# Weight splits after the norms, transfers on another queue and a norm factor applied later, in a two-part transformer on one core

## The chip, the cores and the metric

The kernel runs on one NeuronCore of a Trainium2 chip. Its engines are TensorE (PE: matmuls and their weight loads), VectorE (DVE), ScalarE (ACT) and GpSimd (POOL). SyncE (SP) only issues transfers; GpSimd, ScalarE and SyncE each have a queue of transfers that are issued in order. The metric is the device time of one execution in microseconds (us); the time of a kernel is the median of its runs.

## The reference

One sequence of 256 tokens of width 1024 goes through two layers (differential attention with PEER, then stick-breaking attention with PEER), then through one block of a second network, all in fp32. Cut to the parts that the change touches:

```python
def _layer_norm(x, g, b):
    mu = jnp.mean(xf, axis=-1, keepdims=True)
    var = jnp.mean(jnp.square(xf - mu), axis=-1, keepdims=True)
    return (xf - mu) * lax.rsqrt(var + LN_EPS) * g + b

def rms_norm(x, gain):
    return xf * lax.rsqrt(jnp.mean(xf * xf, axis=-1, keepdims=True) + NORM_EPS) * gain

# first_block, for each of two layers:
    x = _layer_norm(DEEPNORM_ALPHA * x + mix, ln_g[layer, 0], ln_b[layer, 0])
    ffn = _peer(x, ...)              # per token: 128 of 16384 experts, h = gelu(x . u_e), sum of gate h v_e
    x = _layer_norm(DEEPNORM_ALPHA * x + ffn, ln_g[layer, 1], ln_b[layer, 1])

# second_block:
    u = rms_norm(h, attn_pre_norm[l])
    mix = hybrid_mixer(u, ...)       # w_in, attention with rotary step, a recurrence, w_out
    h = h + rms_norm(mix, attn_post_norm[l])
    u = rms_norm(h, mlp_pre_norm[l])
    m = jnp.square(jax.nn.relu(u @ w_mlp_up[l])) @ w_mlp_down[l]
    h = h + rms_norm(m, mlp_post_norm[l])
```

## The kernel before

**Tiles and splits.** All weights come as tiles of 128x1024 fp32 (512 KB). `Stream` loads them in the order of use, on SyncE's queue, into a ring of four raw buffers (L50), and splits each into two rounded parts: `hi`, a copy on ScalarE (L66), and `lo`, the rest, on VectorE (L67). Activations are split the same way (`part`, L163 and L164), and each product is three matmuls, hi·hi, hi·lo and lo·hi (L157 to L159 in `mm3`, L182 in `mm_n`). `next()` hands out a tile and first asks for loads three tiles ahead and for splits two tiles ahead, more if `extra` is set. A split needs a buffer of the parts pool, which has three, or a buffer of its own, which `keep` gives to named tiles. The engines run in program order: the place of `next()` in the code fixes where a split stands on VectorE and ScalarE.

**PEER.** It is computed densely: 128 tiles of `peer_u` give the scores and hidden values of all experts, then a v loop of 128 iterations (in `peer`) takes one tile of `peer_v` each, makes the iteration's weights (`weigh`, L856, and their two parts `wh` and `wo`) and adds to four accumulators in PSUM: two blocks b of 128 tokens by two halves of 512 columns. From iteration GSPLIT = 112 on, tiles may have buffers of their own. In the last DEFER = 6 iterations only the matmuls of block 0 run; those of block 1 are held and run afterwards, while block 0 is normalised. `proj_n`, the other projection onto the model's width, defers in the same way.

**The junction between two stages.** When block 0's accumulators are done, `layer_norm` runs `norm` for block 0: sum with the residual (L305), statistics, centring and gain (L313), root (`rsqrt`), x (L316). TensorE transposes the result (`transposed`, L289), and ScalarE and VectorE split the transposed x into `xh` and `xl`. Then `half_pass(0)` runs block 0 through the first four tiles of the next stage (NJ = 4, the junction tiles; each is used twice, so each has a buffer of its own), 24 matmuls, while block 1 is normalised; its transposes and `half_pass(1)` over the same tiles follow. The four `next()` calls stand in `half_pass(0)`. With `after`, a pre-norm follows the norm at once; so it is after the second PEER, where block 2 begins.

**Block 2.** `proj_n` with w_out ends in the same kind of junction, written out in `block2`: `post_norm` (squares of the accumulator on ScalarE L908, product with the gain L938, root, x = x + u·r at L942), then `pre_norm` of the new x (squares, products with the gain L921 and L923, root, scaling L925), transposes, half passes. x is stored to DRAM at L1208 and loaded again at L1218 into memory that becomes free after the half passes. The MLP has 32 tiles of `w_up`; each projection goes through a relu on ScalarE (L1237), a square and a split. `proj_n` with w_down and a last `post_norm` write `out`.

**What sets the order.** The schedule is written by hand: each engine and each queue runs in the order of the code. Loads of x, gains, masks, keys, cos and sin, and the stores of x between the stages (`spill`), are issued on SyncE's queue, in a row with the weight tiles. A transfer there is issued when all before it have been and when its buffer is free.

## Time and profile before

| | before |
|---|---|
| median of 3 runs | 2309.69 us (2308.02 to 2313.12) |
| the profiled execution | 2311.31 us |
| its span in the trace | 2309.2 us |
| mean granted TensorE clock | 0.988 |
| TensorE busy | 2230.4 us, 97% |
| VectorE, ScalarE, GpSimd busy | 76%, 54%, 3% |
| DMA | 479.85 MB, mean 208 GB/s |

The span reaches from the first to the last instruction of the profiled execution; 2.1 us of its time lie around it. Busy times are shares of the span. Where TensorE stands still, the timeline shows it as a bracket at the next instruction: how long the engine was idle before it, and whose work it waited for.

### The profile page before, as it was taken

To read this page: it belongs to the slowest core of one execution; us is meant where nothing else is said; L and a number is where in the kernel's file an instruction comes from. 1 tells how busy PE (TensorE), PEld (TensorE's weight loads), DVE (VectorE), ACT (ScalarE), POOL (GpSimd) and SP (SyncE) were. 2 spreads that over 40 slices of the span, in tenths; PEclk is the share of its full clock that TensorE was granted. 3 is DMA by queue.
4 is the path that set the end of the run, shared out by engine and by line. 5 is a ranking of instruction groups with operands and counts; after the bars stand their busy time and mean duration, and the time that the engine had idled before them with its cause. 6 is when DMAs were issued, how large, how long until landed. Compare 5 with 4: busy or idle time off the path is not lost.

```text
span 2309.2 us, 39787 instructions
## 1 busy us (share of the span) xinstructions
PE 2230.4 (97%) x15028; PEld 2011.0 (87%) x15028; DVE 1752.8 (76%) x3488; ACT 1237.7 (54%) x2128; POOL 58.3 (3%) x79
## 2 busy tenths in 40 slices
PE   7889999999999999999999999999999899998998
PEld 6769999999888888887999999888888779997987
DVE  5968999888766767576998988766666856676754
ACT  4545454666555444584445566655444546755543
POOL 5400000000000000000000000000000000000000
PEclk9999999999999999999999999999999999999999
DMA  6336667555777777545666655677777564464764
GB/s 209 120 129 226 226 228 241 191 200 203 259 241 259 241 245 252 167 132 179 229 228 229 226 191 201 234 241 243 258 244 249 199 194 149 137 206 142 227 195 142
DMA packets 150657, 479.85 MB, mean 208 GB/s; under 512 B 17728, under 2 KB 18624, under 8 KB 149184
## 3 DMA queue, kind: packets, MB, share of 16 engines
q1 hardware_dynamic: 131456, 442.69, 59.1%
q10 hardware_dynamic: 19008, 34.61, 4.0%
q8 instruction: 118, 1.93, 0.3%
q14 instruction: 75, 0.61, 0.1%
HBM read 437.39 MB, written 39.85 MB: 207 GB/s over the span
## 4 chain that ended last, share of the span: by engine, by line
PE 85%; DVE 6%; ACT 4%; DMA 2%; issue 2%; POOL 1%; SPq 0%; DVEq 0%; ACTq 0%; POOLq 0%
PE ps_acc L182 34%; PE ps_h L157 15%; PE ps_h L159 14%; PE ps_h L158 14%; DVE lo L67 2%; PE ps_acc L805 1%; PE ps_acc L806 1%; ACT hi L66 1%; PE ps_acc L158 1%; PE ps_acc L159 1%; PE ps_acc L157 1%; DMA raw<-w_up 1%; PE ps_acc L689 0%; DVE aa L469 0%; POOL swq L418 0%
## 5 line engine op out<-in xcount | busy, mean ns | idle before, releaser
L67 DVE TENSOR_TENSOR lo<-raw,hi 128x1024 fp32r<-128x1024 f32 x740 | 904.9, 1226 | 454.2 <-ACT hi L66 451.8
L66 ACT CAST hi<-raw 128x1024 fp32r<-128x1024 f32 x740 | 775.4, 1050 | 437.3 <-issue 308.6
L157 PE MATMUL ps_h<-xh,hi 128*128 128x256 f32 x2784 | 790.3, 284 | 5.0 <-ACT r L1237 2.2
L159 PE MATMUL ps_h<-xh,lo 128*128 128x256 f32 x2784 | 774.3, 278 | 1.3 <-DVE lo L67 1.1
L158 PE MATMUL ps_h<-xl,hi 128*128 128x256 f32 x2784 | 774.4, 278 | 0.0
L157 PEld LDWEIGHTS ps_h<-xh,hi 128*128 128x128 f32 x2784 | 526.5, 189 | 11.8 <-ACT r L1237 2.4
L159 PEld LDWEIGHTS ps_h<-xh,lo 128*128 128x128 f32 x2784 | 525.1, 189 | 2.3 <-DVE lo L67 2.3
L158 PEld LDWEIGHTS ps_h<-xl,hi 128*128 128x128 f32 x2784 | 525.3, 189 | 0.2
L182 PE MATMUL ps_acc<-hi,wh 128*128 128x512 f32 x1024 | 315.4, 389 | 3.3 <-ACT wh L163 3.3
L182 PE MATMUL ps_acc<-hi,wo 128*128 128x512 f32 x1024 | 315.4, 389 | 0.0
L182 PE MATMUL ps_acc<-lo,wh 128*128 128x512 f32 x1024 | 315.1, 389 | 0.0
L832 ACT ACTIVATE hs<-ps_h 128x256 f32<-128x256 f32 x256 | 98.3, 384 | 344.1 <-PE ps_h L159 176.2
L182 PEld LDWEIGHTS ps_acc<-hi,wh 128*128 128x128 f32 x1024 | 192.1, 188 | 43.5 <-ACT wh L163 3.6
L182 PEld LDWEIGHTS ps_acc<-hi,wo 128*128 128x128 f32 x1024 | 192.3, 188 | 39.9
L182 PEld LDWEIGHTS ps_acc<-lo,wh 128*128 128x128 f32 x1024 | 192.3, 188 | 39.7
L164 DVE TENSOR_TENSOR wo<-jd,wh 128x256 fp32r<-128x256 f32 x256 | 107.2, 419 | 2.0 <-ACT wh L163 2.0
L856 DVE TENSOR_TENSOR jd<-G,jd 128x256 f32<-128x256 f32 x256 | 106.9, 418 | 2.2 <-ACT G L808 2.2
L163 ACT CAST wh<-jd 128x256 fp32r<-128x256 f32 x256 | 101.7, 397 | 10.4 <-DVE jd L856 10.4
L808 ACT ACTIVATE G<-ps_acc 128x64 f32<-128x64 f32 (+1 forms) x256 | 82.0, 385 | 6.6 <-PE ps_acc L806 1.0
L157 PE MATMUL ps_h<-hi,xh 128*128 128x512 f32 x160 | 70.8, 442 | 11.8 <-ACT hi L66 9.8
L158 PE MATMUL ps_h<-lo,xh 128*128 128x512 f32 x160 | 67.9, 424 | 5.7 <-DVE lo L67 5.7
L159 PE MATMUL ps_h<-hi,xl 128*128 128x512 f32 x160 | 68.0, 425 | 2.5 <-DVE xl L164 2.5
(323 smaller groups left out, 2384.3 us busy)
## 6 DMA issues: line engine op xcount, KB each, us to landing
raw<-peer_u SPq DMA_DIRECT2D x256, 512.0 KB, 4.5
raw<-peer_v SPq DMA_DIRECT2D x256, 512.0 KB, 4.3
H<-hs SPq DMA_DIRECT2D x128, 256.0 KB, 2.1
jd<-H ACTq DMA_DIRECT2D x128, 256.0 KB, 4.2
raw<-w_in SPq DMA_DIRECT2D x32, 512.0 KB, 3.7
raw<-w_up SPq DMA_DIRECT2D x32, 512.0 KB, 4.4
raw<-w_down SPq DMA_DIRECT2D x32, 512.0 KB, 3.7
raw<-w_qkv SPq DMA_DIRECT2D x24, 512.0 KB, 4.5
```

The lines of the kernel that those rows point to most:

```text
L66: self.nc.scalar.copy(hi, raw)
L67: self.nc.vector.tensor_sub(lo, raw, hi)
L157: mm(out, lh, rh, start=start, stop=False)
L158: mm(out, lh, rl, start=False, stop=False)
L159: mm(out, ll, rh, start=False, stop=stop)
L163: self.nc.scalar.copy(hi, src)
L164: self.nc.vector.tensor_sub(lo, src, hi)
L182: mm(acc[half], x, w[:, half * 512 : half * 512 + 512], start=a, stop=b)
L805: mm(out, o[:, 0, j], o[:, 1, j], start=True, stop=False)
L808: nc.scalar.activation(gt[:, :, 4 * g : 4 * g + 4], ps.rearrange("p (t i) -> p i t", t=4)[:, first:end], AF.Copy, scale=1.0 / GSCALE,)
L832: nc.scalar.activation(hs[i // 2][:, i % 2], o, AF.Gelu)
L856: nc.vector.tensor_tensor(w, g[:, i - first], hl[i // 2][:, i % 2], ALU.mult)
```

## The change

Five edits, in the code's order.

- **Splits.** In `half_pass(0)` tiles are taken with `next(calm=True)`, which splits no further than the tile itself; the splits of tiles after the junction move into `half_pass(1)`, one for each tile but the first. One split more is written between the transposes of block 0 and the half pass in `layer_norm` and `block2`. In `peer`'s last 16 iterations and in the last ones of `proj_n`, `extra` rises to 2, so that more junction tiles are split ahead of the norm.
- **Held matmuls** (`finish`): block 1's held jobs run one half of the columns after the other, where before both halves ran job by job.
- **`norm`**: the second half is centred after x of the first half.
- **Queues**: the loads of x, gains, masks, keys, cos, sin and the stores to `spill` are issued on GpSimd's queue. Weight tiles and `out` stay on SyncE's.
- **Block 2's inner norm**: `pre_norm` before the MLP is replaced by the product with its gain, made half by half (`then`). The row factor r of that norm is left out of u; as relu and square follow, the MLP's output lacks r². `late_norm`, after the second half pass, computes r² from x into `factor`, and the last `post_norm` takes it through `by`: as the scale of its squares and as an operand in `rsqrt`.

```diff
-    def next(self):
+    def next(self, calm=False):
...
-        self.split(i + 1 + self.split_ahead + self.extra, i)
+        self.split(i + 1 if calm else i + 1 + self.split_ahead + self.extra, i)
...
+    def finish(self, held):
+
+        for half in range(2):
+            for job in held:
+                self.mm_n(*job, (half,))
...
-            self.st.extra = max(0, min(2, NJ * (k + 2 - count + defer) // defer))
+            self.st.extra = max(0, min(2, k - count + 6))
...
-        for job in held:
-            self.mm_n(*job)
+        self.finish(held)
...
             if b == 0:
-                tiles.append(self.st.next())
+                tiles.append(self.st.next(calm=True))
+            elif j:
+                self.st.split(self.st.used + j, self.st.used)
...
-        nc.vector.tensor_tensor(out, y, z, ALU.mult)
+        if by is None:
+            nc.vector.tensor_tensor(out, y, z, ALU.mult)
+        else:
+            nc.vector.scalar_tensor_tensor(out, y, by, z, ALU.mult, ALU.mult)
...
-        self.nc.sync.dma_start(t, src.unsqueeze(0).to_broadcast([P, D]))
+        self.nc.gpsimd.dma_start(t, src.unsqueeze(0).to_broadcast([P, D]))
...
-        for s in halves:
-            nc.vector.scalar_tensor_tensor(y[:, s], y[:, s], mv[:, 0:1], g[:, s], ALU.subtract, ALU.mult)
...
+        centre(halves[0])
         next(root)
         for s in halves:
+            if s is halves[1]:
+                centre(s)
             nc.vector.scalar_tensor_tensor(x[:, b, s], y[:, s], r, beta[:, s], ALU.mult, ALU.add)
...
+        self.st.split(self.st.used + NJ, self.st.used)
         next(n1)
         self.half_pass(0, tiles)
...
-            nc.sync.dma_start(x, a["x"].rearrange("(b p) d -> p b d", p=P))
+            nc.gpsimd.dma_start(x, a["x"].rearrange("(b p) d -> p b d", p=P))
...
+                if i >= GSPLIT:
+                    self.st.extra = min(2, (i - GSPLIT) // 4)
                 hi, lo = self.st.next()
...
+            nc.scalar.activation(junk, halves[h], AF.Square, scale=1.0 if by is None else by, accum_out=ss[:, h : h + 1])
...
+    def late_norm(self, pool, x, square):
+
+        r = pool.tile([P, 1], F32, tag="lt_r", name=f"ltr{self.n}", bufs=2)
+        yield from self.mean_square(pool, r, [x[:, :512], x[:, 512:]], 1e-6)
+        self.nc.vector.tensor_tensor(square, r, r, ALU.mult)
+        yield
...
             for b in range(NB):
-                self.post_norm(two, acc[b], x[:, b], gains[0])
-                u = self.pre_norm(two, x[:, b], gains[1])
+                u = two.tile([P, D], F32, tag="ln_y", name=f"lnu{b}", bufs=2)
+                scaled = lambda s: nc.vector.tensor_tensor(u[:, s], x[:, b, s], gains[1][:, s], ALU.mult)
+                self.post_norm(two, acc[b], x[:, b], gains[0], then=scaled)
                 for h in range(2):
                     self.transposed(b, h, u)
                 if b == 0:
+                    self.st.split(self.st.used + NJ, self.st.used)
                     self.half_pass(0, tiles)
             self.half_pass(1, tiles)
-            nc.sync.dma_start(spill, x)
+            for b in range(NB):
+                for _ in self.late_norm(two, x[:, b], factor[:, b : b + 1]):
+                    pass
+            nc.gpsimd.dma_start(spill, x)
```

The places at which the order of instructions moves. A row is a line of the kernel, an operation, and out<-in by tile names; numbers at the names count the tiles.

VectorE at the end of the first PEER, from the end of block 1's norm on, before (`lnr`: the norm's root; `xr0`: x; `lo298`, `lo299`: splits of the third and fourth junction tile; `lo300`, `lo301`: of the two tiles after them; `xl`: the split of the transposed x):

```order
L264 TENSOR_TENSOR lnr304_10673<-rsy307_10694,rsz307_10695 128x1
L316 SCALAR_TENSOR_TENSOR xr0_9141<-lny304_10670,lnr304_10673,gains301_10278 128x512 x2
L67 TENSOR_TENSOR lo298_10710<-raw298_10596,hi298_10709 128x1024
L67 TENSOR_TENSOR lo299_10722<-raw299_10707,hi299_10721 128x1024
L67 TENSOR_TENSOR lo300_10734<-raw300_10719,hi300_10733 128x1024
L67 TENSOR_TENSOR lo301_10746<-raw301_10731,hi301_10745 128x1024
L164 TENSOR_TENSOR xl_72<-ps_m310_10755,xh_71 128x4x128
L164 TENSOR_TENSOR xl_72<-ps_m311_10762,xh_71 128x4x128
```

and now, from the last iteration of the v loop (`wo0127`) to the first sums of block 0's norm (`lny302`), and again from the end of block 1's norm on:

```order
L164 TENSOR_TENSOR wo0127_10578<-jd_73,wh0127_10577 128x256
L67 TENSOR_TENSOR lo298_10597<-raw298_10594,hi298_10596 128x1024
L67 TENSOR_TENSOR lo299_10609<-raw299_10606,hi299_10608 128x1024
L316 SCALAR_TENSOR_TENSOR lny302_10658<-xr0_9141,ps_acc297_7633 128x512
...
L329 SCALAR_TENSOR_TENSOR xr0_9141<-lny304_10680,lnr304_10683,gains301_10278 128x512
L323 SCALAR_TENSOR_TENSOR lny304_10680<-lny304_10680,lnm304_10682,gains301_10278 128x512
L329 SCALAR_TENSOR_TENSOR xr0_9141<-lny304_10680,lnr304_10683,gains301_10278 128x512
L164 TENSOR_TENSOR xl_72<-ps_m310_10747,xh_71 128x4x128
L164 TENSOR_TENSOR xl_72<-ps_m311_10754,xh_71 128x4x128
L67 TENSOR_TENSOR lo300_10769<-raw300_10723,hi300_10768 128x1024
L67 TENSOR_TENSOR lo301_10779<-raw301_10731,hi301_10778 128x1024
```

The third and fourth junction tiles (`lo298`, `lo299`), split after block 1's norm before, are now split before block 0's, and the splits of the tiles after the junction stand behind the split of x.

VectorE at block 2's inner norm, block 0, before (`qnu`, `qnr`: the outer norm; `pnu`, `pnr`, `mss`, `rsx`, `rsz`: the inner norm, its root and sums; `lo680`, `lo681`: splits):

```order
L942 SCALAR_TENSOR_TENSOR x2_23751<-qnu750_24209,qnr750_24208,x2_23751 128x512 x2
L921 TENSOR_TENSOR pnu751_24229<-x2_23751,gains736_23753 128x512
L910 TENSOR_TENSOR mss751_24231<-mss751_24231 128x1
L260 TENSOR_SCALAR rsx751_24236<-mss751_24231 128x1
L923 TENSOR_TENSOR pnu751_24229<-x2_23751,gains736_23753 128x512
L262 SCALAR_TENSOR_TENSOR rsz751_24238<-rsy751_24237,rsx751_24236 128x1
L263 TENSOR_SCALAR rsz751_24238<-rsz751_24238 128x1
L264 TENSOR_TENSOR pnr751_24228<-rsy751_24237,rsz751_24238 128x1
L925 TENSOR_SCALAR pnu751_24229<-pnu751_24229,pnr751_24228 128x512
L164 TENSOR_TENSOR xl_72<-ps_m753_24248,xh_71 128x4x128
L164 TENSOR_TENSOR xl_72<-ps_m754_24255,xh_71 128x4x128
L67 TENSOR_TENSOR lo680_24280<-raw680_24269,hi680_24279 128x1024
```

and now (`lnu0`: x times the inner norm's gain):

```order
L966 SCALAR_TENSOR_TENSOR x2_23755<-qnu750_24214,qnr750_24213,x2_23755 128x512
L1230 TENSOR_TENSOR lnu0_24212<-x2_23755,gains736_23757 128x512
L966 SCALAR_TENSOR_TENSOR x2_23755<-qnu750_24214,qnr750_24213,x2_23755 128x512
L1230 TENSOR_TENSOR lnu0_24212<-x2_23755,gains736_23757 128x512
L164 TENSOR_TENSOR xl_72<-ps_m752_24235,xh_71 128x4x128
L164 TENSOR_TENSOR xl_72<-ps_m753_24242,xh_71 128x4x128
L962 TENSOR_TENSOR qnu754_24282<-ps_acc749_24056,gains736_23757 128x512
```

The inner norm's sums and root are gone, x and its product with the gain alternate by halves, and no split stands before block 1's outer norm (`qnu754`).

SyncE's queue around the end of block 2's junction, before (`raw`: weight tiles; `xs`: x in DRAM; `x3`: the MLP's copy):

```order
L50 DMA raw680_24269<-w_up2 128x1024
L50 DMA raw681_24277<-w_up2 128x1024
L50 DMA raw682_24289<-w_up2 128x1024
L1208 DMA xs_1657<-x2_23751 128x2048
L1218 DMA x3_24396<-xs_1657 128x2048
L270 DMA gain760_24398<-mlp_post_norm_2 128x1024
L50 DMA raw683_24401<-w_up2 128x1024
L50 DMA raw684_24437<-w_up2 128x1024
```

and now on SyncE's queue and, behind it, what is on GpSimd's from block 2's load of x to the end:

```order
L50 DMA raw680_24256<-w_up2 128x1024
L50 DMA raw681_24264<-w_up2 128x1024
L50 DMA raw682_24272<-w_up2 128x1024
L50 DMA raw683_24407<-w_up2 128x1024
L50 DMA raw684_24439<-w_up2 128x1024
```

```order
L1209 DMA x2_23755<-xs_1661 128x2048
L288 DMA gains736_23757<-attn_post_norm_2 128x1024
L288 DMA gains736_23757<-mlp_pre_norm_2 128x1024
L1241 DMA xs_1661<-x2_23755 128x2048
L1251 DMA x3_24402<-xs_1661 128x2048
L281 DMA gain760_24404<-mlp_post_norm_2 128x1024
```

The store and the load of x and the load of the gain no longer stand between the weight tiles `raw682` and `raw683`.

## Rows read from the trace of the kernel before

**Rows 1.** The page's busy times: us, share of the span, instructions.

```profile
PE 2230.4 (97%) x15028; PEld 2011.0 (87%) x15028; DVE 1752.8 (76%) x3488; ACT 1237.7 (54%) x2128; POOL 58.3 (3%) x79
```

**Rows 2.** Timeline, TensorE after layer 0: start, us, what, [idle before <-releaser].

```profile
141.27 0.72 PE L182 MATMUL ps_acc<-hi,oh 128*128 128x512 f32 x2 [2.14 <-ACT oh L163]
...
150.67 1.82 PE L289 MATMUL ps_m<-ident,x 128*128 128x128 f32 x8 [2.29 <-DVE x L316]
...
162.01 0.50 PE L159 MATMUL ps_h<-hi,xl 128*128 128x512 f32 x1 [1.09 <-DVE xl L164]
```

**Rows 3.** Timeline, TensorE after the first PEER and after layer 1.

```profile
929.33 0.50 PE L157 MATMUL ps_h<-hi,xh 128*128 128x512 f32 x1 [1.53 <-ACT hi L66]
932.44 0.73 PE L158 MATMUL ps_h<-lo,xh 128*128 128x512 f32 x1 [2.60 <-DVE lo L67]
...
1065.93 0.50 PE L159 MATMUL ps_h<-hi,xl 128*128 128x512 f32 x1 [1.41 <-DVE xl L164]
```

**Rows 4.** Timeline, TensorE after the second PEER and at block 2's start.

```profile
1828.98 1.09 PE L289 MATMUL ps_m<-ident,pnu 128*128 128x128 f32 x8 [1.68 <-DVE pnu L925]
...
1838.27 0.79 PE L158 MATMUL ps_h<-lo,xh 128*128 128x512 f32 x1 [2.61 <-DVE lo L67]
...
1844.25 1.06 PE L289 MATMUL ps_m<-ident,pnu 128*128 128x128 f32 x8 [0.93 <-DVE pnu L925]
...
1858.36 0.51 PE L158 MATMUL ps_acc<-lo,xh 128*128 128x512 f32 x1 [0.95 <-DVE lo L67]
```

**Rows 5.** Timeline, TensorE around block 2's inner norm.

```profile
2112.83 1.33 PE L289 MATMUL ps_m<-ident,pnu 128*128 128x128 f32 x8 [4.33 <-DVE pnu L925]
...
2125.05 1.94 PE L289 MATMUL ps_m<-ident,pnu 128*128 128x128 f32 x8 [3.77 <-DVE pnu L925]
...
2145.64 0.39 PE L157 MATMUL ps_h<-xh,hi 128*128 128x256 f32 x1 [2.20 <-ACT r L1237]
```

**Rows 6.** Windows: stretch, us, busy times (instructions) by engine, granted clock, DMA share, GB/s.

```profile
2112.80:2117.00 4.20, 4.17 (x15) 3.15 (x16) 2.60 (x4) 3.59 (x6) 0.00 (x0) 0.59 0.00 0
2117.00:2121.50 4.50, 4.28 (x19) 3.12 (x17) 3.95 (x10) 1.54 (x7) 0.00 (x0) 1.00 0.00 0
2125.00:2131.00 6.00, 5.95 (x19) 4.85 (x20) 1.38 (x2) 1.80 (x4) 0.00 (x0) 0.53 0.05 22
...
1838.00:1843.00 5.00, 4.73 (x11) 3.47 (x11) 4.97 (x9) 1.79 (x6) 0.00 (x0) 0.50 0.74 208
```

**Rows 7.** Timeline, VectorE at the end of the first PEER.

```profile
915.41 1.27 DVE L305 SCALAR_TENSOR_TENSOR lny<-xr,ps_acc 128x512 f32<-128x512 f32 x2
...
931.17 4.62 DVE L67 TENSOR_TENSOR lo<-raw,hi 128x1024 fp32r<-128x1024 f32 x4
```

**Rows 8.** Timeline, ScalarE in the first PEER's last iterations.

```profile
908.72 1.05 ACT L66 CAST hi<-raw 128x1024 fp32r<-128x1024 f32 x1 [0.95 <-DMA raw<-peer_v]
```

**Rows 9.** Timeline, VectorE at block 2's inner norm, block 0.

```profile
2108.50 1.42 DVE L942 SCALAR_TENSOR_TENSOR x<-qnu,qnr,x 128x512 f32<-128x512 f32 x2
2109.83 0.69 DVE L921 TENSOR_TENSOR pnu<-x,gains 128x512 f32<-128x512 f32 x1
```

**Rows 10.** Timeline, SyncE's queue behind block 2's junction: time and issue of a transfer.

```profile
2122.07 0.33 SPq L1208 DMA_DIRECT2D xs<-x  x1
2134.53 0.33 SPq L1218 DMA_DIRECT2D x<-xs  x1
```

**Rows 11.** The chain of work that ended last, in order of time: start, us, what.

```profile
2135.38 8.55 DMA raw<-w_up
```

**Rows 12.** Windows, the start; columns as in rows 6.

```profile
6.00:8.00 2.00, 0.01 (x1) 0.01 (x1) 0.39 (x2) 1.10 (x2) 0.00 (x0) 1.00 1.03 405
```

**Rows 13.** Timeline, VectorE at the end, block 1's last norm.

```profile
2301.95 1.41 DVE L938 TENSOR_TENSOR qnu<-ps_acc,gain 128x512 f32<-128x512 f32 x2 [4.03 <-ACT msj L908]
```

**Rows 14.** The page's DMA issues: out<-in, queue, count, KB each, median us to landing.

```profile
raw<-peer_v SPq DMA_DIRECT2D x256, 512.0 KB, 4.3
...
x<-x SPq DMA_DIRECT2D x1, 1024.0 KB, 6.1
```

More of the change, by code (lines that the diff above doesn't have):

```diff
@@ L175, in proj_t, with mm_n @@
         return o
-    def mm_n(self, acc, xh, xl, hi, lo, start, stop):
+    def mm_n(self, acc, xh, xl, hi, lo, start, stop, halves=range(2)):
         mm = self.nc.tensor.matmul
         for x, w, a, b in ((xh, hi, start, False), (xh, lo, False, False), (xl, hi, False, stop)):
-            for half in range(2):
+            for half in halves:
                 mm(acc[half], x, w[:, half * 512 : half * 512 + 512], start=a, stop=b)
+    def finish(self, held):
+        for half in range(2):
+            for job in held:
+                self.mm_n(*job, (half,))
     def proj_n(self, xh, xl, count, pool, defer, ready=None):
@@ L251, in half_pass, with rsqrt @@
             self.passed = []
-    def rsqrt(self, pool, out, v, eps, scale=1.0):
+    def rsqrt(self, pool, out, v, eps, scale=1.0, by=None):
         nc = self.nc
@@ L276, in gains @@
         for i, src in enumerate(srcs):
[L277 removed]
+            load = lambda i=i, src=src: self.nc.gpsimd.dma_start(t[:, i], src.unsqueeze(0).to_broadcast([P, D]))
             if late is None:
@@ L890, in peer @@
                         held.append(job)
-            for job in held:
-                self.mm_n(*job)
+            self.st.extra = 0
+            self.finish(held)
             vctx.close()
@@ L899, in peer, with mean_square @@
             gctx.close()
-    def mean_square(self, pool, out, halves, eps):
+    def mean_square(self, pool, out, halves, eps, by=None):
         nc = self.nc
@@ L907, in mean_square @@
         for h in range(2):
-            nc.scalar.activation(junk, halves[h], AF.Square, accum_out=ss[:, h : h + 1])
+            nc.scalar.activation(junk, halves[h], AF.Square, scale=1.0 if by is None else by, accum_out=ss[:, h : h + 1])
         yield
         nc.vector.tensor_tensor(ss[:, 0:1], ss[:, 0:1], ss[:, 1:2], ALU.add)
-        yield from self.rsqrt(pool, out, ss[:, 0:1], eps, 1.0 / D)
+        yield from self.rsqrt(pool, out, ss[:, 0:1], eps, 1.0 / D, by)
     def pre_norm(self, pool, x, gain):
@@ L927, in pre_norm, with post_norm @@
         return u
-    def post_norm(self, pool, acc, x, gain, out=None):
+    def late_norm(self, pool, x, square):
[3 more added lines that the diff above has]
+        yield
+    def post_norm(self, pool, acc, x, gain, out=None, by=None, then=None):
         nc = self.nc
@@ L934, in post_norm @@
         halves = [slice(0, 512), slice(512, D)]
-        root = self.mean_square(pool, r, acc, 1e-6)
+        root = self.mean_square(pool, r, acc, 1e-6, by)
         next(root)
@@ L944, in post_norm @@
                 nc.sync.dma_start(out[:, s], x[:, s])
+            if then:
+                then(s)
     def softplus_neg(self, pool, out, lam):
@@ L968, in block2 @@
         mm = nc.tensor.matmul
-        outer = ExitStack()
+        outer, ctx_f = ExitStack(), ExitStack()
+        fp = ctx_f.enter_context(tc.tile_pool(name="b2f", bufs=1))
+        factor = fp.tile([P, NB], F32, tag="factor", name="factor")
         keep = outer.enter_context(tc.tile_pool(name="b2o", bufs=1))
@@ L979, in block2 @@
             sin = one.tile([P, NB, 16], F32, tag="sin", name="sin2")
-            nc.sync.dma_start(cos, a["c_cos2"])
-            nc.sync.dma_start(sin, a["c_sin2"])
+            nc.gpsimd.dma_start(cos, a["c_cos2"])
+            nc.gpsimd.dma_start(sin, a["c_sin2"])
             cv = one.tile([P, KD, 8], F32, tag="cv", name="cv2")
-            nc.sync.dma_start(cv, a["cols2"])
+            nc.gpsimd.dma_start(cv, a["cols2"])
             mask = one.tile([P, W], F32, tag="mask", name="mask2")
-            nc.sync.dma_start(mask, a["c_mask2"])
+            nc.gpsimd.dma_start(mask, a["c_mask2"])
             qk = [self.jd, kn]
@@ L1241, in block2 @@
             for b in range(NB):
-                self.post_norm(two, acc[b], x[:, b], gain, a["out"][b * P : b * P + P])
+                self.post_norm(two, acc[b], x[:, b], gain, a["out"][b * P : b * P + P], factor[:, b : b + 1])
+        ctx_f.close()
 def body(tc, a, stop="all"):
```

26 lines of the change are left out of this document (13 added, 13 removed).

## The prediction

> **What bounds the kernel now.** I read the busy times first: TensorE is busy for 2230.4 us, 97% of the 2309.2 us span, and VectorE for 76% [rows 1]. So an edit that only relieves VectorE or ScalarE pays nothing, unless it ends one of the waits in which TensorE stands still; all of these together are about 79 us. I therefore read TensorE's timeline for the bracketed waits and kept those in the stages that the diff touches. They stand where a norm must be finished on VectorE before TensorE can transpose its result: after layer 0 (2.14, 2.29 and 1.09 us) [rows 2], after the first PEER and after layer 1 (1.53, 2.60, 1.41) [rows 3], after the second PEER and at the start of block 2 (1.68, 2.61, 0.93, 0.95) [rows 4], and around block 2's inner norm (4.33, 3.77, 2.20) [rows 5]. The releaser named in the bracket tells two kinds apart: a norm's result that is late (x, pnu, xl), and a weight tile whose split is late (hi L66, lo L67).
>
> Then the windows, for the clock. After some of these stops TensorE's granted clock falls from 2.4 to 1.2 GHz for a while: between 2117 and 2121.5, 19 matmuls of a half pass took 4.28 us at a clock of 1.00, 0.225 each, and from 1838 on 11 took 4.73 us at 0.50, 0.43 each [rows 6]. So a half-speed matmul of this shape costs 0.2 us more, and a wait costs more than its bracket.
>
> **The inner norm of block 2.** This is the largest term. Block 0: TensorE stopped at 2112.83 - 4.33 = 2108.50, and x came from 2108.50 on, 0.71 us a half [rows 5, 9]. What then filled the time to 2112.83 was the pre-norm's squares, its root and its scaling. Now only the multiplication by the gain stands there, 0.69 us a half, in turn with x's halves. First half ready at 2108.5 + 0.7 + 0.7 = 2109.9, a wait of 1.4; second half at 2111.3, of which four transposes (half of 1.33 us) hide 0.7, so 0.7 more. 4.33 becomes 2.1: gain 2.2. Block 1: its norm began behind two splits, some 1.2 us each [rows 7], which now come after it, and it loses the same 4.33 - 0.7 - 0.7 = 2.9 us of pre-norm. TensorE reaches its transposes after a half pass of 24 x 0.225 = 5.4 us. The norm's own chain needs about that and the second half's 0.7: I leave 0.7 of the 3.77 us, gain 3.1. Clock: after the two stops it stood at 0.59 for 4.2 us and at 0.53 for 6 us [rows 6], which is 4.2 x 0.41 + 6 x 0.47 = 4.5 us lost. With waits of 1.4 and 0.7 I count half of it, gain 2.2 (0 to 4.5).
>
> The third wait, 2.20 us, is a transfer's. A w_up tile was issued at 2135.38 and took 8.55 us [rows 11]. On SP's queue it stood behind the store of x (2122.07, which waits for the norm) and the load of x (2134.53, which waits for memory that the half pass frees) [rows 10]. Both move to GpSimd's queue with the gain, so the tile is there in time. In its place come the factor's squares and roots, ahead of ScalarE's first relu: the first projection's bank is released later. Cost between 0 (ScalarE idles there otherwise) and the 2.2; I take 0.7, gain 1.5. All of this: 2.2 + 3.1 + 2.2 + 1.5 = 9.0, from 5 to 12.
>
> Here the rows show the queue's order as the cost: the tile is issued 0.85 us after the load of x that it stands behind, and not before. The Trainium skill, DMA: Bandwidth & Descriptors, section "Issuing engines are not separate DMA queues", speaks against the move: it says that transfers of all issuers run on the same 16 engines and that a second issuer saves issue time only. By that rule alone the 1.5 us would be 0 and the sum 1.5 smaller. No row contradicts the sharing; what the rule leaves out is the wait in front of the issue.
>
> **After the first PEER.** VectorE finished x of block 1 and only then made four splits, 931.17 to 935.8 [rows 7], while TensorE waited 1.53 and 2.60 us for the third junction tile [rows 3] and then, by its timeline, ran nine matmuls at half speed: 4.1 + 9 x 0.2 = 5.9 us. The four junction tiles are now cut before the norm. This is not free. Two splits more, 1.2 us each, stand in the last iterations of the v loop, between the products that TensorE waits for, and each needs its transfer: the ring has four buffers, and a late tile already held ScalarE up for 0.95 us [rows 8]. A ring turn is one landing (4.3 us [rows 14]), one ScalarE copy of 1.05 and one split of 1.2; by that the fourth tile is cut about 3.4 us later than the norm began before, 915.41, and TensorE's last iterations slip by up to 2. TensorE did not wait for block 0's norm, which began at 915.41 [rows 7]: its timeline has no bracket there before the one at 929.33. So this norm has some slack, and its delay costs little beyond that slip. I give back 1.9: gain 4.0, from 2 to 6. The reordered centring brings x's first half 0.7 us earlier and its second half not at all, so it helps only where the first half is what is waited for.
>
> **After the second PEER.** The same edit, but here the norm is longer (a pre-norm follows at once) and TensorE was already waiting for it, 1.68 us [rows 4]. The delay of 3.4 less the slip of 2 makes that 3.0; the wait for splits (2.61 and the half-speed stretch of 12 matmuls, 2.4 us) goes, but the pre-norm of block 1, freed of four splits (4.6 us), still ends about 2.3 us after the half pass, where 0.93 us were waited before: 1.4 more. Slip -2.0, first wait -1.4, splits +2.6, clock +2.4, second wait -1.4 make 0.2; I take 0, from -2 to 3. The 0.95 us at 1858.36, a split behind the rotary step that waits for cos and sin, is covered by the three splits now made during the second half pass: 0.5, from -1 (cos and sin later on the other queue) to 1.
>
> **After layer 0 and layer 1.** In layer 0 one split moves ahead into an idle stretch of ScalarE, so that the last head's part comes about 1.0 us earlier (the 2.14). The 2.29 becomes about 1.6 for the first half and 0.8 between the halves, but matmuls start 1.3 us earlier, since the eight transposes (1.82) overlap it; the 1.09, for xl behind two splits, goes: 0.9 net. 3.2, from 1 to 4.5. After layer 1 the same cause gives most of 1.41: 1.3, from 0.5 to 1.8.
>
> **The end.** VectorE's two products at 2301.95 took 1.41 us after the last matmul [rows 13]. With all first halves ahead of the second ones, one product and one square of block 1 are done before; the other half remains: 0.7. The squared factor enters as an operand, in instructions that were there: 0.
>
> **The start.** The load of x, 1024 KB [rows 14], was issued behind the first tiles; on GpSimd's queue nothing holds it back. Between 6 and 8 us TensorE makes the first 0.01 us of its work, having waited for its first tile, and the DMA engines are at 1.03 busy and 405 GB/s [rows 12]. 1 MB at that rate is 2.6 us: the loss lies between 0 (x starts late) and 2.6 (x goes first); I take the middle, 1.3. Of other moved transfers (gains, masks, keys, the later loads of x) I count nothing: they are asked for tens of us before their use; where one came late, its norm would wait for it microsecond for microsecond.
>
> **Sum.** 9.0 + 4.0 + 0 + 0.5 + 3.2 + 1.3 + 0.7 - 1.3 = 17.4 us. The profiled execution took 2311.31 us (span 2309.2 and 2.1 around it), 1.6 above the median of 2309.69. 2311.3 - 17.4 = 2293.9, and for a median run 2292.
>
> **Rivals.** (a) The early splits cost what they save: in both v loops ring and VectorE are tight, TensorE slips more, the norms start later still. Then the first PEER's term is 0 and the second's -3: 17.4 - 7 = 10.4, time 2299. For it: 0.95 us of waiting for a tile already. Against it: VectorE is idle for 24% of the span. Chance 0.15. (b) No half-speed stretch survives, and x at the start disturbs nothing: block 2 gains 2.2 more, the second PEER 3, layer 0 1, the start 1.3: 24.9, time 2285. Chance 0.11. (c) Slower: GpSimd's queue delivers late. At the start of block 2 cos and sin stand behind the store of x on it, VectorE waits for them, and every later split waits behind VectorE. Three splits in hand cover about 8 us (12 matmuls of 0.225 to a tile); beyond them each microsecond is one of TensorE's. It takes 22 us to end above 2314, a landing about 30 us after issue, where x's load of 1 MB took 6.1 [rows 14]; time 2315. Chance 0.03. The Trainium skill, SBUF - State Buffer, section "SBUF: two separate sides", has a rule of that kind: descriptors for GpSimd's transfers are written by GpSimd's cores, which some VectorE modes lock out. No run here shows such a transfer; (c) stands without it. (d) The waits move and nothing is won: the rows name many releasers, and all would have to be replaced; time 2309. Chance 0.04.
>
> **How the numbers follow.** The forecast has 0.67. A measurement of this kernel tells 0.2%, 4.6 us, from no change. Faster: 0.67 + 0.15 + 0.11 = 0.93; same 0.04; slower 0.03. The range takes in (a) and (b) and the bounds of block 2's term: 2284 to 2301.
>
> **What would show it.** In the profile of the changed kernel: at block 2's norm waits near 1.4 and below 1 instead of 4.33 and 3.77; no w_up issue at the load of x; after the first PEER no wait for lo L67, with xl ahead of the splits; after the second PEER a first wait near 3; the first matmul at 8 to 10 us. Wrong it would be if waits of several us on a transfer of GpSimd's queue appear, or if TensorE waits for wh or wo in the last iterations of the v loops for more than 2 us.

## The result, and the profile after

The changed kernel takes **2293.95 us** (median of 6 runs, 2291.54 to 2296.89), the kernel before 2309.0 us (6 runs). The ratio is 0.9929, 95% interval 0.9914 to 0.9944: 15 us, 0.7%, less. The forecast was 2292 with a range from 2284 to 2301.

Its profiled execution took 2291.54 us, span 2289.7. The page's first rows:

```profile
span 2289.7 us, 39872 instructions
PE 2221.8 (97%) x15028; PEld 2002.0 (87%) x15028; DVE 1755.3 (77%) x3488; ACT 1238.3 (54%) x2126; POOL 77.3 (3%) x114
```

Against [rows 1], VectorE and ScalarE do the same work, and GpSimd issues the transfers that it was given. TensorE's timeline at the places of [rows 2 to 5] (start, duration, instruction, [idle before <-releaser]):

```profile
17.71 0.50 PE L158 MATMUL ps_h<-lo,xh 128*128 128x512 f32 x1 [0.65 <-DVE lo L67]
...
141.47 0.74 PE L182 MATMUL ps_acc<-hi,oh 128*128 128x512 f32 x2 [1.00 <-ACT oh L163]
149.99 0.66 PE L300 MATMUL ps_m<-ident,x 128*128 128x128 f32 x4 [1.39 <-DVE x L329]
151.44 0.66 PE L300 MATMUL ps_m<-ident,x 128*128 128x128 f32 x4 [0.79 <-DVE x L329]
...
928.84 0.63 PE L300 MATMUL ps_m<-ident,xr 128*128 128x128 f32 x4 [0.49 <-DVE xr L329]
...
1045.57 0.63 PE L300 MATMUL ps_m<-ident,x 128*128 128x128 f32 x4 [1.28 <-issue]
1047.06 0.95 PE L300 MATMUL ps_m<-ident,x 128*128 128x128 f32 x4 [0.86 <-DVE x L329]
...
1820.73 1.09 PE L300 MATMUL ps_m<-ident,pnu 128*128 128x128 f32 x8 [2.84 <-DVE pnu L942]
1831.93 1.62 PE L300 MATMUL ps_m<-ident,pnu 128*128 128x128 f32 x8 [2.47 <-DVE pnu L942]
...
2096.27 0.66 PE L300 MATMUL ps_m<-ident,lnu 128*128 128x128 f32 x4 [2.14 <-DVE lnu L1230]
2097.75 0.63 PE L300 MATMUL ps_m<-ident,lnu 128*128 128x128 f32 x4 [0.82 <-DVE lnu L1230]
2106.64 0.50 PE L157 MATMUL ps_h<-hi,xh 128*128 128x512 f32 x1 [0.24 <-ACT xh L163]
```

No wait for a split is left at a junction. The waits on norms are there still. After layer 0 and at block 2's inner norm they are shorter and cut into halves; after the second PEER both have grown, from 1.68 to 2.84 and from 0.93 to 2.47; after layer 1 the two halves (1.28 and 0.86) add up to more than the one wait of 1.45 before. The wait of 2.20 for a w_up tile has no row any more.

One wait is new. ScalarE, then TensorE, where layer 1 begins:

```profile
940.91 0.40 ACT L563 CAST tri<-tri_in 128x256 fp32r<-128x256 f32 x1 [3.85 <-DMA tri_in<-c_tri]
941.23 0.37 ACT L626 COPY k<-ps_h 128x256 f32<-128x256 f32 x1
```

```profile
941.64 0.39 PE L157 MATMUL ps_h<-xh,hi 128*128 128x256 f32 x1 [1.05 <-ACT k L626]
```

`tri_in` is one of the masks that moved to GpSimd's queue, behind the store of x. It was issued at 934.65, ScalarE waited 3.85 us for it, the copy of `k` stands behind it on ScalarE, and TensorE waited 1.05 us for that copy. All ten kept executions that have the moved splits and the moved mask show this wait of TensorE, 0.65 to 1.51 us; none of the four that lack one of the two has it. With the splits alone the mask was issued on SyncE's queue at 932.41 and was there when ScalarE came to it at 936.92.

A second execution of the same kernel (after_again, below) had a span of 2296.5. The spans of the first two profiles, 2309.2 and 2289.7, differ by 19.5 us where the medians differ by 15, so they flatter the change by some 4 us, and I read both executions of the changed kernel. The table takes from TensorE's timelines when each stage's first matmul starts; a stage's gain is its length before less its length after.

| stage | forecast | gain, first profile | gain, second |
|---|---|---|---|
| start to the first output projection | -1.3 | -1.3 | -1.5 |
| that, and layer 0's junction | 3.2 | 3.5 | 3.4 |
| u loop of the first PEER | 0 | 1.7 | 0.0 |
| its v loop and junction | 4.0 | 5.1 | 5.0 |
| layer 1 and its junction | 1.3 | 0.3 | -1.4 |
| u loop of the second PEER | 0 | 1.2 | 0.4 |
| its v loop, junction, and 512-column part of w_in | 0.5 | 2.5 | 0.5 |
| rest of block 2 to w_out | 0 | 1.8 | 1.9 |
| w_out, inner norm, up projection | 9.0 | 6.9 | 6.4 |
| down projection | 0 | -2.1 | -2.1 |
| last norm (from the end of the last matmul) | 0.7 | 0.0 | 0.0 |
| sum | 17.4 | 19.5 | 12.7 |

### The profile page after: what moved, and what is told of

Same layout as the page of the kernel before. It is cut to its first block, busy times and chain, and to the rows that moved or that the text cites. A ratio compares the mean times of both kernels' runs of the same rounds, so it can differ in the third digit from the quotient of the medians.

```text
span 2289.7 us, 39872 instructions
## 1 busy us (share of the span) xinstructions
PE 2221.8 (97%) x15028; PEld 2002.0 (87%) x15028; DVE 1755.3 (77%) x3488; ACT 1238.3 (54%) x2126; POOL 77.3 (3%) x114
## 4 chain that ended last, share of the span: by engine, by line
PE 82%; DVE 6%; issue 4%; ACT 4%; DMA 2%; POOL 1%; ACTq 0%; DVEq 0%; POOLq 0%
PE ps_acc L182 31%; PE ps_h L157 15%; PE ps_h L159 14%; PE ps_h L158 14%; DVE lo L67 2%; ACT hi L66 1%; PE ps_acc L819 1%; PE ps_acc L820 1%; PE ps_acc L159 1%; PE ps_acc L158 1%; PE ps_acc L157 1%; DMA xt<-xT 0%; PE ps_acc L703 0%; DVE aa L483 0%; POOL swq L432 0%
## 5 line engine op out<-in xcount | busy, mean ns | idle before, releaser
L819 PE MATMUL ps_acc<-oh 128*128 128x128 f16 x512 | 69.6, 221 | 0.0
L820 PE MATMUL ps_acc<-oh 128*128 128x128 f16 x512 | 68.5, 219 | 0.0
```

The costliest lines, as they stand in the source:

```text
L819: mm(out, o[:, 0, j], o[:, 1, j], start=True, stop=False)
L820: mm(out, o[:, 0, j], o[:, 2, j], start=False, stop=True)
```

## The experiments

**The parts alone, and the changed kernel again.** Three kernels are the kernel before with one part each: the inner norm (with `late_norm`, `by`, `then` and `factor`), the queues, the moved splits (with `extra`, without `finish` and without the new order in `norm`). The edits are those of the diff above, for the queues no more than

```
-nc.sync.dma_start(...)
+nc.gpsimd.dma_start(...)
```

> The kernel before with the edit of block 2's inner norm alone (late_norm, factor, product with the gain by halves); queues, splits and order stay as before. By the prediction's terms: the first wait (4.33 us) becomes about 2, the second (3.77) keeps the two splits of 2.4 us in front of block 1's norm and becomes about 1, half-speed matmuls halve; the wait of 2.20 for a w_up tile stays, since store and load of x stay on SyncE's queue. Gain 5 to 7 us, time 2302 to 2304. Rival, waits only move: what was behind the norm waits instead, gain under 2 us, 2307 or more. On the matmul pace in the MLP (256 columns each 0.113 us before, 0.118 after the whole change): if the slower pace comes from the memory layout (the new small factor tile), it is 0.118 here; if it comes from where and how TensorE was stopped before, this run may show either, and 0.113 speaks against the layout.

Measured: 2311.7 against 2313.57 us for the kernel before, ratio 1.0 (0.999 to 1.0011). TensorE's timeline:

```profile
2105.46 0.66 PE L292 MATMUL ps_m<-ident,lnu 128*128 128x128 f32 x4 [1.82 <-DVE lnu L1216]
2106.93 0.63 PE L292 MATMUL ps_m<-ident,lnu 128*128 128x128 f32 x4 [0.82 <-DVE lnu L1216]
2115.65 0.63 PE L292 MATMUL ps_m<-ident,lnu 128*128 128x128 f32 x4 [0.93 <-DVE lnu L1216]
2117.04 0.63 PE L292 MATMUL ps_m<-ident,lnu 128*128 128x128 f32 x4 [0.76 <-DVE lnu L1216]
...
2139.02 0.58 PE L157 MATMUL ps_h<-xh,hi 128*128 128x256 f32 x1 [4.96 <-ACT r L1255]
```

The waits at the norm fell, from 4.33 and 3.77 to 2.64 (1.82 and 0.82) and 1.69 (0.93 and 0.76), a little less than forecast, and the sum is nothing: the wait for the w_up tile grew from 2.20 to 4.96, and both projections of the MLP ran slower (below). The rival, waits only move, holds for this part alone.

> The kernel before with the transfers moved to GpSimd's queue alone. By the prediction's terms: the first matmul comes 0.6 us later and some 1.3 us are lost by the first output projection; the wait of 2.20 us for a w_up tile goes (+1.5 to 2.2); cos and sin move the wait of 0.95 by up to 1 either way. Sum -0.5 to +1.5, time 2307.5 to 2309.5. Rival, the queue order is no cost because all queues share the same engines: the 2.20 stays, sum -1.3, 2310 or more. Rival, GpSimd's queue delivers late: waits of several us for x or cos and sin, 2312 or more. MLP pace 0.113 expected, since neither layout nor stops before it change.

Measured: 2307.48, ratio 0.9979 (0.9969 to 0.9988). The 2.20 is gone, the norm's waits stay, and one wait, at 17.52, is new:

```profile
17.52 0.50 PE L158 MATMUL ps_h<-lo,xh 128*128 128x512 f32 x1 [0.54 <-DVE lo L67]
...
2108.95 1.65 PE L289 MATMUL ps_m<-ident,pnu 128*128 128x128 f32 x8 [4.23 <-DVE pnu L925]
2121.49 1.94 PE L289 MATMUL ps_m<-ident,pnu 128*128 128x128 f32 x8 [4.16 <-DVE pnu L925]
```

No wait of TensorE for x, cos or sin appears, so rival (c) has nothing behind it here. But the gain isn't seen where it was forecast: the up projection ran at its slower pace (below) and gave most of the 2.20 back, and in the trace 3.4 of the 3.8 us lie in the u loops, which also differ between executions of one kernel.

> The kernel before with the moved splits alone (calm, half_pass(1), extra in the v loops and the projections); held matmuls, norm's order, queues and block 2's inner norm stay. By the prediction's terms: after the first PEER waits of 1.53 and 2.60 go and about 1 to 2 us are lost in the v loop's last iterations, +4; after the second PEER about +2 as measured in the changed kernel; layer 0 +1 to 2 (the 2.14 and the 1.09); block 2's second norm +2.4 (its two splits come later). Sum 7 to 10 us, time 2299 to 2302. Rival, the gain there needs the reordered centring and the half-major held matmuls too: then the norms are late, waits on x stand where waits on lo stood, sum under 4, 2305 or more.

Measured: 2298.26, ratio 0.9944 (0.9924 to 0.9964). This part alone carries most of the gain, and neither `finish` nor the order in `norm` is needed for it. In time the three parts add up to 0.77%, about the whole, so these two edits, which no run has by themselves, bring nothing that the times show. What the splits alone leave:

```profile
1819.73 1.97 PE L291 MATMUL ps_m<-ident,pnu 128*128 128x128 f32 x8 [3.13 <-DVE pnu L931]
1831.31 1.07 PE L291 MATMUL ps_m<-ident,pnu 128*128 128x128 f32 x8 [3.37 <-DVE pnu L931]
...
2109.74 1.07 PE L291 MATMUL ps_m<-ident,pnu 128*128 128x128 f32 x8 [2.04 <-DVE pnu L931]
...
2128.67 0.39 PE L157 MATMUL ps_h<-xh,hi 128*128 128x256 f32 x1 [2.15 <-ACT r L1244]
```

> The changed kernel once more, unaltered: which of its features return in another execution. If the matmul pace in the MLP (0.118 us for 256 columns, 0.233 for 512 until the last six tiles) belongs to the program, it returns to within 0.001; if it is chance of one execution, it is 0.113 and 0.227 here and the time is 4 us less or the slower pace stands elsewhere. Time 2291 to 2297 either way; the waits after the PEERs (2.84, 2.47) and at block 2's norm (2.14, 0.82) return within 0.2 us.

Measured: 2293.84, ratio 0.9916 (0.99 to 0.9933). The MLP's slower pace returned; the first wait after the second PEER was 4.33 instead of 2.84, so my 0.2 us there was wrong, and the u loops took 1.7 and 0.8 us longer than in the first execution with the same instructions in the same order.

**Early splits.** The changed kernel without

```diff
-                if i >= GSPLIT:
-                    self.st.extra = min(2, (i - GSPLIT) // 4)
```

> The changed kernel without the extra splits in the last 16 iterations of both v loops (the two lines that set extra there); the rest of the change stays. Theory: the v loops' ends come 1.1 us earlier and the first wait after the second PEER falls from 2.8 or more to about 1.7; but the third and fourth junction tile are split behind block 1's norm again, waits of about 1.5 and 2.6 us on hi and lo and half-speed matmuls return at both places: +4.9 at the first, +1 to 4 at the second, time 2299 to 2303. Rival (a) of the prediction, the early splits cost what they save: no difference, 2292 to 2296.

Measured: 2294.64, ratio 0.9928 (0.9911 to 0.9945). The theory falls: no wait on hi or lo came back. VectorE at block 1's norm after the first PEER, and TensorE after both PEERs:

```profile
923.47 0.68 DVE L164 TENSOR_TENSOR xl<-ps_m,xh 128x512 fp32r<-128x512 f32 x1
924.07 2.35 DVE L67 TENSOR_TENSOR lo<-raw,hi 128x1024 fp32r<-128x1024 f32 x2
926.34 1.28 DVE L319 BATCH_NORM_STATS2 lns<-lny 128x6 f32<-128x512 f32 x2
```

```profile
930.16 0.63 PE L300 MATMUL ps_m<-ident,xr 128*128 128x128 f32 x4 [1.75 <-DVE xr L329]
...
1822.55 1.09 PE L300 MATMUL ps_m<-ident,pnu 128*128 128x128 f32 x8 [2.07 <-DVE pnu L940]
...
1836.04 1.94 PE L300 MATMUL ps_m<-ident,pnu 128*128 128x128 f32 x8 [4.87 <-DVE pnu L940]
```

The two splits now stand ahead of block 1's statistics: the call of `split` between the transposes and the half pass sees to that, not `extra`. They delay the norm instead of the half pass, by 1.75 and 4.87 us where the changed kernel waits 0.49 and 2.47. Against that, block 0's transposes come 1.1 and 1.8 us earlier than with the early splits. By the traces the early splits win some 1 us net at the first PEER (v loop and junction gained 4.0 here, 5.0 to 5.1 with them) and nothing clear at the second (1.4 here, 0.5 and 2.5 with them); in the time neither shows.

**The queue behind block 2's junction.** The changed kernel with three transfers put back:

```
-nc.gpsimd.dma_start(spill, x)     # store behind the half passes, load of x3, gain
+nc.sync.dma_start(spill, x)
```

> The changed kernel with three transfers back on SyncE's queue: the store of x behind block 2's junction, its load for the MLP and the last gain. Theory: the weight tiles of the MLP stand behind them again, TensorE waits 2 to 5 us at the third or a later tile of the up projection (4.96 where the norm was changed alone); then the time is 2296 to 2299. If a stop of TensorE sets the pace of what follows, the up projection runs at 0.113 behind it instead of 0.118 (some 25 tiles x 24 x 0.0045 = 2.7 us back) and the net is 0 to +2. Rival, the shared engines make the queue's order indifferent: no wait, 2294.

Measured: 2300.09, ratio 0.9954 (0.994 to 0.9968). SyncE's queue, the last instruction of `late_norm` on VectorE, then TensorE:

```profile
2107.61 0.33 SPq L1241 DMA_DIRECT2D xs<-x  x1
2120.60 0.33 SPq L1251 DMA_DIRECT2D x<-xs  x1
2120.98 0.42 SPq L1254 DMA_DIRECT2D gain<-mlp_post_norm  x1
2121.45 11.86 SPq L50 DMA_DIRECT2D raw<-w_up  x6
```

```profile
2120.24 0.16 DVE L950 TENSOR_TENSOR factor<-ltr 128x1 f32<-128x1 f32 x1
```

```profile
2130.53 0.58 PE L157 MATMUL ps_h<-xh,hi 128*128 128x256 f32 x1 [6.62 <-ACT r L1272]
```

The load of x is issued 13 us after the store, right behind the end of `late_norm`; the weight tiles stand behind it in the queue, and TensorE waits 6.62 us; the up projection, from its first 256-column matmul to the down projection's first, is 5.9 us longer (85.9 against 80.0). The rival is out.

**The load of x at the start.**

```diff
-            nc.gpsimd.dma_start(x, a["x"].rearrange("(b p) d -> p b d", p=P))
+            nc.sync.dma_start(x, a["x"].rearrange("(b p) d -> p b d", p=P))
```

> The changed kernel with the first load of x back on SyncE's queue, behind the weight tiles. Theory: its 1 MB no longer competes with the first weight tiles; the wait of 0.65 to 0.76 us for a split at 17.7 us goes and the first output projection begins 0.6 to 1.3 us earlier, time 2293. Rival, the start's loss is not this transfer's (gains and others, or chance): the wait stays and the time too, 2294.

Measured: 2291.03, ratio 0.9918 (0.9898 to 0.9937), an interval that overlaps the changed kernel's. The wait at 17.7 us is gone and the first output projection starts at 115.1 instead of 116.3. At layer 0's junction 1.3 us are lost again. Windows from 150 to 156 us (columns as in [rows 6]) of the changed kernel and of this one show to what:

```profile
150.00:156.00 6.00, 5.14 (x24) 3.84 (x25) 5.89 (x12) 1.67 (x4) 0.00 (x0) 1.00 0.01 3
```

```profile
150.00:156.00 6.00, 5.70 (x20) 4.31 (x21) 5.83 (x14) 1.22 (x4) 0.00 (x0) 0.72 0.01 3
```

After waits of the same length (1.39 and 0.79; 1.43 and 0.80) the granted clock stayed at 1.00 in one execution and fell in the other. That needn't be the edit's doing: from the last matmul of the output projection to the end of the second half pass the clock was 1.00 in both executions of the changed kernel (16.9 us), and 0.91 in all eight of its variants (18.1 to 18.3 us), in four of which nothing up to there is edited.

**The pace in the MLP.** By the windows, the changed kernel runs the up and the down projection without waits and at a granted clock of 1.00, as the kernel before does, and yet does fewer matmuls. Before, 50 us of the up projection and 60 of the down projection (the first two numbers in brackets count matmuls and weight loads), then after:

```profile
2150.00:2200.00 50.00, 50.00 (x443) 50.00 (x443) 37.70 (x58) 31.26 (x58) 0.00 (x0) 1.00 0.69 202
2220.00:2280.00 60.00, 60.00 (x267) 49.69 (x266) 27.65 (x23) 25.01 (x24) 0.00 (x0) 1.00 0.63 198
```

```profile
2130.00:2180.00 50.00, 50.00 (x427) 50.00 (x426) 34.99 (x54) 28.86 (x54) 0.00 (x0) 1.00 0.64 190
2200.00:2260.00 60.00, 60.00 (x259) 48.31 (x258) 26.96 (x23) 23.83 (x23) 0.00 (x0) 1.00 0.65 190
```

443 matmuls of 256 columns against 427 (from start to start 0.113 and 0.118 us), 267 of 512 columns against 259 (0.227 and 0.233). The down projection had 259 in the kernel with the new norm alone and 267 and 266 in the two other parts, so this loss belongs to the norm's edit. What that edit moves besides the norm is memory: `factor`, 8 bytes in each partition, takes 32 as it is allocated, and all that block 2 allocates lies that much further, uh and ul among it, while the weight tiles stay.

```diff
-        factor = fp.tile([P, NB], F32, tag="factor", name="factor")
+        factor = fp.tile([P, 32], F32, tag="factor", name="factor")[:, :NB]
```

> The changed kernel with its factor tile made 128 bytes long per partition instead of 8; nothing else. In the changed kernel everything allocated behind the factor lies 32 bytes further than before, and in the down projection a 512-column matmul takes 0.233 us until the last six tiles, 0.227 in the kernel before. Theory, the place in memory sets this pace: with 128 bytes the down projection is back at 0.227 throughout, 312 matmuls x 0.0067 = 2.1 us less, time about 2292. Rival, the pace comes from the order of work (other norm, other stops): it stays 0.233 and the time 2294. The up projection's pace (0.118 against 0.113 for 256 columns) is not tied to this, since its operands lie where they lay before: 0.118 again by this theory, 0.113 if it is chance.

```profile
2200.00:2260.00 60.00, 60.00 (x260) 48.64 (x259) 27.21 (x24) 24.49 (x24) 0.00 (x0) 1.00 0.62 190
```

Measured: 2293.57, and 260 matmuls: no. With `[P, 128]` in place of `[P, 32]`, 512 bytes:

> The changed kernel with its factor tile made 512 bytes long per partition. 128 bytes left the down projection at 0.232 to 0.233 us a matmul, so the theory as first put fell; what the kernel before, with its 0.227, and the last six tiles have in common is that the two operands, weight tile and activation, begin at the same place counted in blocks of 512 bytes. Theory, that place sets the pace: with 512 bytes the operands agree again, 0.227 throughout the down projection, 2.1 us less than the changed kernel, about 2292. Rival, the order of work sets it and the new norm is the cause: 0.233 again until the last tiles, 2294.

```profile
2200.00:2260.00 60.00, 60.00 (x266) 49.69 (x266) 28.33 (x24) 25.05 (x24) 0.00 (x0) 1.00 0.66 195
```

Measured: 2291.93, ratio 0.9911 (0.9895 to 0.9928), 266 matmuls, and the down projection is 2.1 us shorter. The same instructions in the same order run at 0.233 or 0.227 by where uh and ul lie. The changed kernel has a control in itself: the last six tiles of the down projection have their buffers in one pool with uh and ul and moved with them, and they ran at 0.227, the 26 tiles before them at 0.233. The up projection, whose operands didn't move, stayed at 427.

> The changed kernel with the 512-byte factor and with the first load of x on SyncE's queue. The two gains lie in different stages (down projection 2.1 us; first output projection 1.0 us earlier) and should add: about 3 us less than the changed kernel, 2290 to 2291. Rival: the gain at the start is lost again at the first norm, which begins earlier with a different grant of the clock (1.3 us were lost there when x was moved alone): 2292.

Measured: 2290.77, ratio 0.9908 (0.9891 to 0.9924), the best time of all. Its interval overlaps that of the changed kernel, so by time alone it isn't told from it; the trace has the 2.1 us in the down projection. Then the same with a gap behind the constants, of 192 bytes and of 64:

```diff
+        self.gap = c.tile([P, 48], F32, tag="gap", name="gap")
```

> As the run with both edits, and 192 unused bytes behind the constants, so that every weight tile lies at another place relative to the transposed activations (256 bytes apart in blocks of 512 instead of 64). The 256-column matmuls of the PEERs' first halves and of the up projection run at either 0.113 or 0.118 us and change between the two in the same kernel. Theory, place: with another distance the pace of these stages is another and steadier one; at 0.113 throughout it would save up to 8000 x 0.0014 = 11 us, at 0.120 (as where the attention's output meets its weights at equal places) it costs up to 40 us. Rival, only the history of stops sets it for these stages: a mixture of 0.113 and 0.118 as before, time as the run with both edits within 2 us.

> As the run with the gap of 192 unused bytes, with 64 instead. There the weight tiles lay 256 bytes apart from the transposed activations, counted in blocks of 512, and every 256-column matmul took 0.120 us, as where both lie at equal places; at 64 bytes apart the pace was 0.113 or 0.118. Here they lie 128 apart, the farthest from both. Theory, place, and the farther from equal in blocks of 256 the better: 0.113 throughout, the mean falls from 0.1142 to 0.1133, 8000 x 0.0009 = 7 us less than the run with both edits, 2283 to 2286. Rival, any change of the 64 bytes found by the kernel before is a loss: 0.118 or 0.120 throughout, 30 to 45 us more, 2320 or more. Rival, 128 behaves as 64: a mixture, 2290 to 2292.

Measured: 2326.27, ratio 1.0056 (1.0039 to 1.0073), and 2325.32, ratio 1.0067 (1.005 to 1.0084). The up projection without the gap, with 192 and with 64 bytes:

```profile
2130.00:2180.00 50.00, 50.00 (x443) 50.00 (x443) 36.81 (x55) 29.50 (x55) 0.00 (x0) 1.00 0.65 197
```

```profile
2170.00:2220.00 50.00, 50.00 (x419) 50.00 (x418) 34.42 (x52) 28.26 (x53) 0.00 (x0) 1.00 0.59 184
```

```profile
2170.00:2220.00 50.00, 50.00 (x423) 50.00 (x423) 34.60 (x54) 28.88 (x54) 0.00 (x0) 1.00 0.58 183
```

419 and 423 where 443 were: 192 or 64 bytes that nothing reads cost 35 us. By the traces (41 and 39 us longer than the one of the kernel without the gap, an execution 6 us below its median) 15 to 16 of it lie in each u loop, most of the rest in block 2's projections and the up projection. The down projection kept its pace, with 192 bytes:

```profile
2240.00:2300.00 60.00, 60.00 (x266) 49.70 (x265) 28.84 (x24) 25.07 (x24) 0.00 (x0) 1.00 0.66 200
```

There uh lies behind the gap as the weight tiles do, while xh lies ahead of it. So a pace changed where one of TensorE's two operands moved, and didn't where both moved together. That farther apart is better is refuted; that any other place than the one found is a loss held for both that were tried.

## Why the prediction was right, point by point

- **What bounds the kernel.** Right: VectorE and ScalarE do as much as before, and the gain is TensorE's. Of the 19.5 us of the first profile 10.9 are idle time that is gone (78.8 to 67.9 us) and 8.6 are busy time, half-speed stretches (mean granted clock 0.988 to 0.993) and pace.
- **Block 2's inner norm.** The first wait was forecast at 1.4 and 0.7 by halves and is 2.14 and 0.82; the second at 0.7 and is 0; the third, of 2.20, goes. The queue's order was worth more than the 1.5 I gave it: put back, it costs 5.9 us, because the load of x now waits for `late_norm` as well. The Trainium skill, DMA: Bandwidth & Descriptors, section "Issuing engines are not separate DMA queues", says that a second issuer saves only the time to initiate a transfer, and by that rule alone the term is 0. These runs differ: the 13 us between the two issues of x above are a wait on the queue ahead of the issue. By the traces norm and queue need each other: from w_out to the end of the up projection the norm alone lost 3.9 us and the queue alone 0.1, the whole change gained 6.4 to 6.9. The term of 9.0 was too large all the same, since the up projection ran at 0.118, and the down projection, forecast at 0, lost 2.1. "The squared factor enters as an operand, in instructions that were there: 0" is the step that failed: its 8 bytes cost 2.1 us, by where they push uh and ul.
- **After the first PEER.** Forecast 4.0, measured 5.0 to 5.1: the v loop ended 1.1 to 1.2 us late (forecast up to 2) and the junction won 6.2. (The forecast passed over a bracket of 0.24 us at 924.48, for xh; nothing hangs on it.) But the cause was put in the wrong place, in part. I took the early splits for what removes the waits on lo; the call of `split` ahead of the half pass removes them, and the early splits add some 1 us in the traces and nothing in the times.
- **After the second PEER.** The first wait was forecast at 3.0 and is 2.84 and 4.33, the second at 2.3 and is 2.47 and 2.23. The net of 0.5 and 2.5 us lies within -3 to 4, the two ranges given added up.
- **Layer 0** gave 3.4 to 3.5 of 3.2. That it is so near is partly luck: 1.3 of it hang on the clock, which stayed up at this junction in both executions of the changed kernel and in none of its eight variants, where output projection and junction gained 2.2 to 3.9.
- **Layer 1** gave 0.3 and -1.4 of 1.3. The mechanism was right: xl no longer waits (1.41). From the last matmul of the output projection to the end of the second half pass the time went from 18.1 us to 16.7 with the splits alone and to 16.3 to 16.8 in the five variants in which the clock stayed at 1.00. In both executions of the changed kernel it fell (0.91 and 0.90) and took the gain back: 18.0 and 17.9. So whether the new order in `norm` gains here isn't settled. What the forecast left out is the mask: of the other moved transfers it counted nothing, since they are asked for tens of us before their use; `tri_in` was used 6.3 us after its issue, and TensorE's wait of 1.05 and 1.15 us is the price.
- **The end.** Nothing of 0.7. VectorE's first product does run early, but the second waits for ScalarE's square of the second half, which with the factor as its scale takes 0.69 us where it took 0.60:

```profile
2282.83 0.69 DVE L962 TENSOR_TENSOR qnu<-ps_acc,gain 128x512 f32<-128x512 f32 x1 [3.44 <-ACT msj L925]
```

The last step, x, begins 3.0 us after the end of the last matmul instead of 3.2, and the span ends no earlier behind that matmul (7.8 us both times).

- **The start.** -1.3 to -1.5 of -1.3. The transfer of x is the cause of the wait at 17.7: all seven kept executions with x on GpSimd's queue have one, of 0.29 to 0.76 us, and none of the seven with x on SyncE's. What else is lost there differs from one execution to the next: the first output projection starts at 114.6 to 116.8 in the former and at 113.5 to 115.7 in the latter, 1.2 us apart on the mean.
- **The rivals.** (a) holds for what it names: without the early splits the time is the same (2294.64 against 2293.95). Its 2299 didn't come, since the splits that matter are others. (b) failed, since both kinds of loss in it are there. (c) did not occur as told: VectorE waited 6.65 us for cos, as before (6.59), and TensorE not behind it; but one of the signs of being wrong appeared, a wait of several us on a transfer of GpSimd's queue, in `tri_in`. (d) did not occur. Right was the sum, 17.4 against 15, by terms that were off in both directions; that they nearly cancel is luck.

Left open: why 256-column matmuls at the place found by both kernels run at 0.113 in some stretches and 0.118 in others of the same program (427 or 443 in the up projection of one kernel or another, with and without a stop before it, and the u loops differ between executions). A stop was followed by 0.113 in three kernels (2.15, 2.20 and 6.62 us) and by 0.118 in one (4.96), so stops alone don't set it. `finish` and the new order in `norm` were not tried by themselves.

## What to carry to other kernels

A norm that TensorE waits for gains from what is cut ahead of it or behind it more than from its own instructions; move both the splits and the transfers, and look at which queue the next tile stands in before shortening the norm. A transfer that waits for another engine's work doesn't belong on the queue of the weights, but look at how soon after its issue each moved transfer is used. And compare the count of matmuls per window in stages that the change doesn't touch: a few bytes more in an early pool can move every later tile.

## What was not expected of the hardware

TensorE's pace at a granted clock of 1.00 depends on where its two operands lie relative to each other. In the down projection, with the weight tiles at one place, 512-column matmuls took 0.227 us with uh at the place of the kernel before or 512 bytes behind it, 0.233 at 32 and 0.232 at 128 bytes; they took 0.227 again where uh and the weights had moved together. In the up projection and the u loops, 256-column matmuls took 0.113 to 0.118 with the first layout and 0.118 to 0.120 when the weight tiles' buffers lay 64 or 192 bytes further from xh. The Trainium skill, TensorE: Matmul & The Clock Gate, section "Step-by-step: what each phase is for", says that TensorE reads the streaming operand and the weights through two independent ports, so that loading weights doesn't take read bandwidth from the running matmul. By that rule alone the distance between the two would not matter, and here it makes up to 6%. That the two reads are what meets is argued from this and not shown, and which of the two waits for which no run here shows.
